# A hybrid attention block on one core: late weights split in place, eleven gate buffers, an earlier attention start and held transposes

## The chip, the cores and the metric

The kernel runs on 1 core of one Trainium2 chip. The metric is the device time of one execution in microseconds (us), the median over several runs. The engines are named as in the profile: PE (TensorE, matmuls) with PEld (its weight loads), DVE (VectorE), ACT (ScalarE), POOL (GpSimd), and SP (SyncE), on whose queue the kernel issues nearly all of its DMA transfers. Each engine works through its own instructions in order and waits for the others by semaphores.

## The reference

One layer over 2048 rows of 1024 numbers, float32. All inputs are projected at once, three branches follow, each with its own gate, and one output projection with a residual and a norm closes:

```python
h = rms_norm(x, norm_g)
z = h @ w_in
(aq, ak, av, af, az, bq, bk, bv, ba, bb, bz, mq, mz, gates) = _split_cols(z, IN_SIZES)
o_a = forgetting_attention(q, k, v, af + b_fg)          # 8 heads of 64, causal, 2048 x 2048
y_a = o_a * silu(az)
o_b = gated_delta_rule(gq, gk, gv, g_log, beta)         # 4 heads of 128, chunked scan
y_b = rms_norm(o_b, gdn_norm_g) * silu(bz)
y_m = memory_attention(mq, mem) * silu(mz)              # 4 heads of 128 over 256 memory rows
proj = einsum('bsnc,ncd->bsnd', [y_a, y_b, y_m], w_branch)   # 3 x (512 -> 1024)
merged = sum_n sigmoid(gates + b_merge)_n * proj_n
return rms_norm(x + merged @ w_out, final_norm_g)
```

## The kernel before

Every large product is made in three matmuls: each float32 operand is split into a rounded high part and its residue (names ending in `h` and `l`), and high x high, high x residue and residue x high are added in PSUM. The split of a tile is a copy to the high part on ScalarE and a subtraction into the residue on VectorE or POOL.

**Who sets the order.** The program is written by generators ("parts") that yield the time at which their next step may run. A class `Plan` (L25) keeps a modelled time for each engine, the SP queue and the transfers, and always takes the first part that is ready by that model; the dense products come last in the list and fill what is left. What is issued this way then stands in each engine's instruction stream, with some reordering by the layer below. `pl.at(t, f)` runs `f` at a modelled time, `Feed` (L109) keeps a limited number of loads under way, `Stores` (L132) issues stores late, and `behind(engine)` places a step directly after that engine's last instruction. On the chip the order stands and only the waits differ.

**The stages.**
1. `part_norm` (L503) norms the rows of `x` and turns them with PE transposes into `hh`/`hl`, the operands of all input products. The first 512 rows come in two pairs of 128-row tiles (`rms_transposed`, L332, once for `v` = 0 and 1). Beside them `dense` (L1492) starts the first two weight columns on half the rows at a time: `pdf` of pair 0, then of pair 1. The transposes (`ptx`, L371) go to a ring of three PSUM buffers; ScalarE copies a half tile to `hh` (L373), VectorE takes the residue to `hl` (L374), which frees the buffer.
2. `dense` then goes through 64 more columns of `w_in` (`pd_in`, L412 to 414), with the memory branch, the delta rule and, at the end, attention beside it. The last 24 columns are the gates. They are made first for the lower half of the rows (`HA`), then for the upper half (`HB`), in pieces of 512 rows; `ev_gate` (L461) counts the pieces of the upper half in `gates_b` and stores each to DRAM (`dgt`).
3. `part_mem_attn` (L712) makes the memory branch's output, 16 pieces of 128 x 512, and stores each already split, as two tiles (`dym`).
4. `part_fox` (L1159) is the forgetting attention. It starts when the lower gates are done and `gates_b` is 6. `maxima` computes scores for the row maxima (`psm`, L1254), `values` the scores again (`pst`) and the value products (`po`, `pq`, L1413 and 1414); POOL adds up the probabilities (L1374). `prep` and `load_q` load keys, values and queries. The outputs go to `dya`.
5. After the gates, `dense` runs the branch products for the delta rule (`n` = 1) and the memory branch (`n` = 2), each for four row groups `g` of 512 and eight output columns `d` of 128: 64 steps of 12 matmuls (`pbr`, L1625 to 1627, in `branch`). Attention runs beside the first 57 or so. A step needs its weights (`W`), its inputs (`yh`/`yl`), a gate tile `gt` (loaded by `load_gate`, two steps ahead), and for `n` = 2 also the partial sum `pp` of `n` = 1. VectorE multiplies gate and product into `gt` (L1654), POOL adds `pp` (L1658), and `gt` is stored to DRAM (`dpt`) and only then free. Gate tiles have 5 buffers in one pool and, until step (2, 2), 5 more in a second pool `bx`; attention may end only after `bx` is closed.
6. `branch_half` (L1765) does the third branch (attention, `n` = 0) on 256 rows at a time, in pairs of columns (`pba`, L1785 to 1787), with a `gt` and a `pp` per pair, and leaves the merged sum in `mh`/`ml`; three PSUM buffers take turns. `out_half` (L1814) multiplies by `w_out` (`pout`, L1832 to 1834), adds the residual, and norms. The sequence is `branch_half(0)`, `branch_half(1)`, `out_half(0)`, `branch_half(2)`, `out_half(1)`, and so on.

**The late weights.** `w_branch` of attention and `w_out` are loaded and split around the passage from stage 5 to 6. `load_wb` for `n` = 0 loads a raw tile `wbr` from the input into one of four staging buffers (`yr`, two loads under way), casts it to `wbh` (L1579) and subtracts into `wbl` (L1580). `load_y1` stages attention's outputs in `yr` likewise. `load_wo` stages a row block of `w_out` in one of two buffers `ld3`, which the output stage's scratch `jk3` shares.

Of the kernel before, what the change touches and what calls it, by code (L numbers as in the profile page):

```python
# [19 lines left out]
P = 128  # L20
# [191 lines left out]
def tile_trunk(ctx, tc, x, mem, norm_g, w_in, w_v, w_lg, b_fg, b_mg, conv_w, a_log, dt_b,  # L212
# [65 lines left out]
    dwb = [dram.tile([P, 2, 8, 4, P], F32, name=f"dwb{n}") for n in range(3)]  # L278
    dF = dram.tile([2, 8, S], F32, name="dF")
# [45 lines left out]
    state = {"gates_a": False, "gates_b": 0, "fox": False, "wb": False, "bx": False, "pv": 0}  # L325
# [6 lines left out]
    def rms_transposed(pool, load, ntile, g_bc, hi, lo, col0, ring, batch, on_dve=(), parts=1):  # L332

        tend = 0.0
        for t0 in range(0, ntile, batch):
# [23 lines left out]
            for t in range(t0, t0 + batch):  # L359
# [4 lines left out]
                for hf in range(KT // 4):  # L364
                    yield later(t2, ring.when), 0.44
                    pt, kb = ring.take("ptx")
                    pt = four(pt)
                    with behind(mybir.EngineType.PE) if parts > 1 else nullcontext():
                        for a in range(4):
                            k = hf * 4 + a  # L370
                            nc.tensor.transpose(pt[:, a, :], xt[:, k * P:(k + 1) * P], ident)  # L371
# [131 lines left out]
    def part_norm():  # L503
        with tc.tile_pool(name="p0", bufs=2) as p0:
# [207 lines left out]
    def part_mem_attn(n, g, h, qh, ql, tq):  # L712
# [53 lines left out]
        yield later(e - AHEAD, lambda: 0.0 if mem_s["y"] == n else INF), 0.0  # L766
        yh = mp.tile([P, 512], F32, tag="yh", name="yh", bufs=1)
# [390 lines left out]

    def part_fox():  # L1159
        yield (lambda: 0.0 if state["gates_a"] and state["gates_b"] >= 6 else INF), 0.0  # L1160
        ps1.close()
        fs = ExitStack()
# [280 lines left out]
        yield (lambda: 0.0 if state["pv"] == NU and state["bx"] else INF), 0.0  # L1443
# [48 lines left out]
    def dense():  # L1492
        first = state["first"]
        ps0 = []
        for v in range(2):
            cs = slice(256 * v, 256 * v + 256)
            for i in range(2):
# [5 lines left out]
                for k in range(KT):  # L1503
                    mm3k(ps[:, cs], wh, wl, hh[0][:, :, cs], hl[0][:, :, cs], k)
                    if k < KT - 1:
                        yield 0.0, 0.34
                if v == 1:
# [43 lines left out]
        bs, bxs = ExitStack(), ExitStack()  # L1551
        bw = bs.enter_context(tc.tile_pool(name="bw", bufs=1, side="right"))
        bp = bs.enter_context(tc.tile_pool(name="bp", bufs=1, side="right"))
        bx = bxs.enter_context(tc.tile_pool(name="bx", bufs=1))
        src_y = [dya, dyb, dym]
        W = {}

        wb_feed, y_feed = Feed(pl, 2), Feed(pl, 2)

        def load_wb(n, d):  # L1560
# [24 lines left out]
        def load_y1(n, g, k):  # L1585
            cell = []
            if n:
# [319 lines left out]
```

## Time and profile before

| | us |
|---|---|
| median of 3 runs | 2618.22 |
| lowest and highest | 2616.93, 2618.88 |
| the profiled execution | 2617.02 |
| its span, first to last instruction | 2615.3 |
| PE busy in it | 2551.5 |
| POOL busy in it | 1016.9 |

The profile is that of one execution. "Busy" adds up the time in which an engine had an instruction under way. A row of a table by stretch gives the stretch, its length, the busy time of each engine with the number of its instructions, the mean granted clock of TensorE as a share of full speed, the mean busy share of the 16 DMA engines, and GB/s moved. In a timeline a row gives start, duration, engine, source line, operation, output and inputs, size and count, and in brackets the idle time before it with what ended it. Matmuls overlap, so their pace is the distance of starts, not the duration.

### The profile page before, as it was taken

The numbers are of one execution on the slowest core, as the hardware profiler recorded it, in microseconds if no ns is written. First come the engines' busy times: TensorE is split into PE (matmuls) and PEld (weight loads), VectorE is DVE, ScalarE is ACT, GpSimd is POOL, SyncE is SP. The second block draws the span as 40 slices with busy tenths as digits, with TensorE's granted clock in tenths as the row PEclk, the third lists the DMA queues.
The fourth block names the chain that finished last, engine by engine and source line by source line (L and its number), as shares of the span: only waits on it lengthen the run. The fifth ranks groups of instructions, "written<-read, shape, count | busy, mean of one in ns | idle before, by whom it ended". The sixth has DMA issues, their size and how long they took to land. (4 is left out here: it accounts for less than half of the span.)

```text
span 2615.3 us, 36792 instructions
## 1 busy us (share of the span) xinstructions
PE 2551.5 (98%) x12656; PEld 2110.6 (81%) x12656; DVE 1337.0 (51%) x2718; ACT 1103.8 (42%) x2296; POOL 1016.9 (39%) x819
## 2 busy tenths in 40 slices
PE   7999999999999999999999999999999999989998
PEld 6778888788888888888888888788887887768887
DVE  6641566656433337712222247666667776635433
ACT  5531234443475532234444335555565444422211
POOL 0011111221144334243333237777775657862111
PEclk9999999999999999999999999999999999999999
DMA  5123222222365665467665463443336787786332
GB/s 194 62 87 118 76 89 89 93 89 88 127 228 200 204 211 170 129 225 226 204 200 164 147 186 94 116 122 113 97 111 213 207 263 228 246 271 218 129 122 73
DMA packets 314986, 407.27 MB, mean 156 GB/s; under 512 B 63520, under 2 KB 186528, under 8 KB 314799
## 3 DMA queue, kind: packets, MB, share of 16 engines
q1 hardware_dynamic: 314654, 404.65, 48.4%
q8 instruction: 100, 1.64, 0.3%
q14 instruction: 88, 0.71, 0.1%
q10 hardware_dynamic: 144, 0.26, 0.0%
HBM read 246.13 MB, written 158.68 MB: 155 GB/s over the span
## 5 line engine op out<-in xcount | busy, mean ns | idle before, releaser
L412 PE MATMUL pd_in<-hh,wh_in 128*128 128x512 f32 x1856 | 746.1, 402 | 3.2 <-DVE evt L455 2.9
L414 PE MATMUL pd_in<-hh,wl_in 128*128 128x512 f32 x1856 | 728.4, 392 | 1.0
L413 PE MATMUL pd_in<-hl,wh_in 128*128 128x512 f32 x1856 | 726.1, 391 | 0.0
L396 POOL TENSOR_TENSOR wl_in<-wr_in,wh_in 128x1024 fp32r<-128x1024 f32 x84 | 203.9, 2427 | 644.3 <-ACT wh_in L392 633.2
L414 PEld LDWEIGHTS pd_in<-hh,wl_in 128*128 128x128 f32 x1856 | 348.8, 188 | 79.3 <-POOL wl_in L396 4.5
L412 PEld LDWEIGHTS pd_in<-hh,wh_in 128*128 128x128 f32 x1856 | 349.8, 188 | 71.7 <-DVE evt L455 4.3
L413 PEld LDWEIGHTS pd_in<-hl,wh_in 128*128 128x128 f32 x1856 | 350.1, 189 | 64.8
L1374 POOL TENSOR_TENSOR acc<-acc,ph 128x512 f32<-128x512 f32 (+3 forms) x288 | 318.7, 1107 | 75.4 <-ACT ph L1394 57.7
L1394 ACT ACTIVATE ph<-pst 128x512 fp32r<-128x512 f32 (+1 forms) x320 | 170.8, 534 | 183.9 <-PE pst L1388 92.6
L1351 DVE TENSOR_TENSOR plo<-pst,ph 128x512 fp32r<-128x512 f32 (+1 forms) x320 | 191.3, 606 | 83.1 <-ACT pst L1396 79.6
L1396 ACT ACTIVATE pst<-pst 128x512 f32<-128x512 f32 (+1 forms) x320 | 170.8, 534 | 0.0
L1658 POOL TENSOR_TENSOR gt<-gt,pp 128x512 f32<-128x512 f32 x64 | 87.4, 1370 | 180.2 <-DVE gt L1654 147.1
L392 ACT CAST wh_in<-wr_in 128x1024 fp32r<-128x1024 f32 x84 | 88.1, 1049 | 156.6 <-PE pd_in L413 138.7
L1261 DVE TENSOR_REDUCE nmx<-psm 128x1 f32<-128x512 f32 x192 | 128.0, 685 | 32.5 <-PE psm L1254 30.8
L1413 PE MATMUL po<-ph,Vs 128*128 128x512 f32 (+1 forms) x320 | 117.2, 368 | 2.3 <-ACT ph L1394 2.2
L1387 PE MATMUL pst<-QA,KA 128*128 128x512 f32 (+1 forms) x320 | 117.5, 367 | 2.0 <-DVE QA L1269 1.7
L486 DVE SCALAR_TENSOR_TENSOR evv<-xb,cw,evv 128x512 f32<-128x512 f32 x144 | 116.6, 809 | 3.7
L1414 PE MATMUL pq<-plo,Vs 128*128 128x512 f32 (+1 forms) x320 | 116.9, 367 | 0.7 <-DVE plo L1351 0.7
L1388 PE MATMUL pst<-QB,KB 128*128 128x512 f32 (+1 forms) x320 | 117.1, 367 | 0.0
L1254 PE MATMUL psm<-KA,QA 68*128 68x512 f32 (+2 forms) x320 | 109.6, 375 | 4.3 <-DVE nmx L1258 2.0
L1832 PE MATMUL pout<-woh,mh 128*128 128x512 f32 x256 | 101.1, 397 | 8.4 <-ACT mh L1758 6.5
L1625 PE MATMUL pbr<-yh,wbh 128*128 128x512 f32 x256 | 102.1, 399 | 5.9 <-DVE gt L1654 5.3
(353 smaller groups left out, 4750.0 us busy)
## 6 DMA issues: line engine op xcount, KB each, us to landing
wr_in<-in_w_in SPq DMA_DIRECT2D x84, 512.0 KB
dgt<-evg SPq DMA_DIRECT2D x96, 256.0 KB
gt<-dgt SPq DMA_DIRECT2D x96, 256.0 KB
dpt<-gt SPq DMA_DIRECT2D x64, 256.0 KB
pp<-dpt SPq DMA_DIRECT2D x64, 256.0 KB
dgq<-evv SPq DMA_DIRECT2D x48, 256.0 KB
kqv<-dgq SPq DMA_DIRECT2D x16, 768.0 KB
xt<-in_x SPq DMA_DIRECT2D x16, 512.0 KB
```

Of the source, the lines that this page charges most:

```text
L396: nc.gpsimd.tensor_sub(lo, raw, hi.bitcast(F32))
L412: nc.tensor.matmul(ps, wh[:, k, :], xh[:, k, :], start=(k == 0), stop=False)
L413: nc.tensor.matmul(ps, wh[:, k, :], xl[:, k, :], start=False, stop=False)
L414: nc.tensor.matmul(ps, wl[:, k, :], xh[:, k, :], start=False, stop=(k == kt - 1))
L1261: nc.vector.tensor_reduce(mx, ps[:, 0:w], AX.X, ALU.max)
L1351: nc.vector.tensor_sub(plo[:, 0:w], ps[:, 0:w], ph[:, 0:w].bitcast(F32))
L1374: nc.gpsimd.tensor_add(acc[:, c0:512], acc[:, c0:512], ph[:, 0:w].bitcast(F32))
L1387: nc.tensor.matmul(ps[:, 0:w], KA[kt][:, ks], QAn[:, c0:512], start=True, stop=False)
L1388: nc.tensor.matmul(ps[:, 0:w], KB[kt][:, ks], QBn[:, c0:512], start=False, stop=True)
L1394: nc.scalar.activation(ph[:, 0:w], ps[:, 0:w], AF.Exp, scale=0.125)
L1396: nc.scalar.activation(ps[:, 0:w], ps[:, 0:w], AF.Exp, scale=0.125)
L1413: nc.tensor.matmul(po[:, c0:512], V[:, 0:128], ph[:, 0:w], start=(t0 == 0), stop=(t0 == NT - 1))
```

## The change

Seven edits go together:

- The transposes of the second pair of tiles are held until both `pdf` products of the first pair have been issued (`turn`, `state["pair"]`), and placed right behind PE's last instruction.
- For the last row group, the memory branch stores its output whole. `load_y1` splits it when it is loaded.
- `part_copy`, started with attention, copies attention's `w_branch` and `w_out` from the inputs to DRAM tiles `dw0` and `dwo`, one block of each at a time, 30 us of modelled time apart.
- Attention starts when `gates_b` is 3, and its end no longer waits for `bx`.
- Late weights, attention's outputs and the last memory group land in the residue's tile (`wbl`, `wol`, `yl`); ScalarE casts from there to the high part and the residue is subtracted in place. The staging buffers and their feeds go.
- Gate tiles have 11 buffers in one pool from first to last; `bx` is gone.
- `w_out` blocks are asked for two at first, then one with each pair of columns of `branch_half`. `jk3` has a buffer of its own.

```diff
+    def part_copy():
+
+        for d in range(8):
+            with behind(mybir.EngineType.SP):
+                move(dw0[:, d], w_br[0, d], 512)
+                move(dwo[d], w_out[d], 1024)
+            yield pl.pe + 30.0, 0.0
+
     def part_fox():
-        yield (lambda: 0.0 if state["gates_a"] and state["gates_b"] >= 6 else INF), 0.0
+        yield (lambda: 0.0 if state["gates_a"] and state["gates_b"] >= 3 else INF), 0.0
         ps1.close()
+        pl.add(part_copy())
...
-        yield (lambda: 0.0 if state["pv"] == NU and state["bx"] else INF), 0.0
+        yield (lambda: 0.0 if state["pv"] == NU else INF), 0.0
...
-                    yield later(t2, ring.when), 0.44
+                    yield later(t2, ring.when, turn or 0.0), 0.44
...
-                    with behind(mybir.EngineType.PE) if parts > 1 else nullcontext():
+                    with behind(mybir.EngineType.PE) if parts > 1 or turn else nullcontext():
...
+            first_pair = lambda: 0.0 if state["pair"] == 2 else INF
...
-                                                     256 * v, rc, 1, (1,))
+                                                     256 * v, rc, 1, (1,), turn=first_pair if v else None)
...
+        if g == NG - 1:
+            yield e, 0.0
+            move(dym[g][:, h, 0, :], zm, 256, e)
+            mem_s["left"] -= 1
+            mem_s["y"] = n + 1
+            return
...
-            def load():
-                raw = bp.tile([P, 4, P], F32, tag="yr", name="wbr", bufs=4)
-                return raw, move(raw, w_br[n, d], 256)
-
-            def use(raw):
-                hi, lo = tiles()
-                nc.scalar.copy(hi, raw)
-                nc.gpsimd.tensor_sub(lo, raw, hi.bitcast(F32))
+            hi, lo = tiles()
+            t = move(lo.bitcast(F32), dw0[:, d], 256)
+
+            def use():
+                nc.scalar.copy(hi, lo.bitcast(F32))
+                nc.gpsimd.tensor_sub(lo, lo.bitcast(F32), hi.bitcast(F32))
                 cell.extend((hi, lo, pl.pool(512, pl.act(512, pl.pe))))

-            wb_feed.ask(load, use)
+            pl.at(t, use)
...
-            if n:
-                hi = bp.tile([P, 512], F32R, tag="yh", name="yh", bufs=YB)
-                lo = bp.tile([P, 512], F32R, tag="yl", name="yl", bufs=YB)
+            hi = bp.tile([P, 512], F32R, tag="yh", name="yh", bufs=YB)
+            lo = bp.tile([P, 512], F32R, tag="yl", name="yl", bufs=YB)
+            if n and (n, g) != (2, NG - 1):
...
+            t = move(lo.bitcast(F32), src_y[n][g][:, k, 0, :] if n else src_y[n][g][:, k, :], 256)
+            pl.at(t, lambda: cell.extend((hi, lo, split(hi, lo, lo.bitcast(F32), 512, pl.pe))))
             return cell
...
-        YB, GB, GX = 8, 5, 5
+        YB, GB = 8, 11
...
-                wide = n == 1 or g < NG // 2
-                parts.leave(GB + GX * wide - 3)
-                pool, bufs = next(turn) if wide else (bp, GB)
-                gt = pool.tile([P, 512], F32, tag="gt", name="gt", bufs=bufs)
+                parts.leave(GB - 3)
+                gt = bp.tile([P, 512], F32, tag="gt", name="gt", bufs=GB)
...
-            def load():
-                raw = f3.tile([P, D], F32, tag="ld3", name="wor", bufs=2)
-                return raw, move(raw, w_out[k], 512)
+            woh, wol = F["woh"], F["wol"]
+            raw = wol[:, k].bitcast(F32)
+            t = move(raw, dwo[k], 512)
...
-                for k in range(KT):
-                    load_wo(k)
+                for _ in range(2):
+                    load_wo(ks.popleft())
...
-            if (n, g) == (2, NG // 2):
-                parts.leave(0)
-                bxs.close()
-                state["bx"] = True
...
                     load_pair(*todo.popleft())
+                if ks:
+                    load_wo(ks.popleft())
...
-                        jk = f3.tile([P, D], F32, tag="ld3", name="jk3", bufs=2)
+                        jk = f3.tile([P, D], F32, name="jk3", tag="jk3")
```

More of the change, by code (lines that the diff above doesn't have):

```diff
@@ L278, in tile_trunk @@
     dwb = [dram.tile([P, 2, 8, 4, P], F32, name=f"dwb{n}") for n in range(3)]
+    dw0 = dram.tile([P, 8, 4, P], F32, name="dw0")
+    dwo = [dram.tile([P, D], F32, name=f"dwo{k}") for k in range(8)]
     dF = dram.tile([2, 8, S], F32, name="dF")
@@ L324, in tile_trunk @@
     hhalf = [INF] * 2
-    state = {"gates_a": False, "gates_b": 0, "fox": False, "wb": False, "bx": False, "pv": 0}
+    state = {"pair": 0, "gates_a": False, "gates_b": 0, "fox": False, "wb": False, "pv": 0}
     done = {}
@@ L330, in load_x, with rms_transposed @@
         return xt, move(xt, src[row: row + P, :], 512)
-    def rms_transposed(pool, load, ntile, g_bc, hi, lo, col0, ring, batch, on_dve=(), parts=1):
+    def rms_transposed(pool, load, ntile, g_bc, hi, lo, col0, ring, batch, on_dve=(), parts=1, turn=None):
         tend = 0.0
@@ L1506, in dense @@
                         yield 0.0, 0.34
+                state["pair"] += 1
                 if v == 1:
@@ L1592, in load_y1 @@
                 return cell
-            def load():
-                raw = bp.tile([P, 512], F32, tag="yr", name="yr", bufs=4)
-                return raw, move(raw, src_y[n][g][:, k, :], 256)
-            def use(raw):
-                hi = bp.tile([P, 512], F32R, tag="yh", name="yh", bufs=YB)
-                lo = bp.tile([P, 512], F32R, tag="yl", name="yl", bufs=YB)
-                cell.extend((hi, lo, split(hi, lo, raw, 512, pl.pe)))
-            y_feed.ask(load, use)
+            t = move(lo.bitcast(F32), src_y[n][g][:, k, 0, :] if n else src_y[n][g][:, k, :], 256)
+            pl.at(t, lambda: cell.extend((hi, lo, split(hi, lo, lo.bitcast(F32), 512, pl.pe))))
             return cell
@@ L1632, in branch @@
                     mid()
-        gates, parts, turn = {}, Stores(pl), itertools.cycle([(bp, GB)] * GB + [(bx, GX)] * GX)
+        gates, parts = {}, Stores(pl)
         def load_gate(n, g, d, ahead=0):
             if (n, g, d) not in gates:
-                wide = n == 1 or g < NG // 2
-                parts.leave(GB + GX * wide - 3)
-                pool, bufs = next(turn) if wide else (bp, GB)
-                gt = pool.tile([P, 512], F32, tag="gt", name="gt", bufs=bufs)
+                parts.leave(GB - 3)
+                gt = bp.tile([P, 512], F32, tag="gt", name="gt", bufs=GB)
                 move(gt, dgt[g][:, n * 8 + d, :], 256)
@@ L1665, in ev_dram, with use @@
             return e
-        F, wo, wo_feed = {}, {}, Feed(pl, 2)
+        F, wo, ks = {}, {}, collections.deque(range(KT))
         def load_wo(k):
-            f3, woh, wol = (F[n] for n in ("f3", "woh", "wol"))
-            def load():
-                raw = f3.tile([P, D], F32, tag="ld3", name="wor", bufs=2)
-                return raw, move(raw, w_out[k], 512)
-            def use(raw):
+            woh, wol = F["woh"], F["wol"]
+            raw = wol[:, k].bitcast(F32)
+            t = move(raw, dwo[k], 512)
+            def use():
                 nc.scalar.copy(woh[:, k], raw)
@@ L1681, in use @@
                 wo[k] = pl.pool(D, t) if k % 2 else pl.dve(D, t)
-            wo_feed.ask(load, use)
+            pl.at(t, use)
         def open_out():
@@ L1838, in out_half @@
                     if jk is None:
[L1839 removed]
+                        jk = f3.tile([P, D], F32, name="jk3", tag="jk3")
                     nc.scalar.activation(jk[:, cs], xt[:, cs], AF.Square, accum_out=s2[:, hf:hf + 1], scale=D ** -0.5)
                     if row == S - P and not hf:
[L1842 removed]
+                        xf = jk[:, cs]
                         nc.gpsimd.tensor_mul(xf, xt[:, cs], fg[:, cs])
[L1844 removed]
                     e = pl.act(512, e)
```

6 lines of the change are left out of this document (1 added, 5 removed).

## The prediction

> **What bounds the kernel now.** I read the page first, then the stretches by engine, the waits of TensorE, and the timelines of the two places where it stands.
>
> ```profile
> span 2615.3 us, 36792 instructions
> PE 2551.5 (98%) x12656; PEld 2110.6 (81%) x12656; DVE 1337.0 (51%) x2718; ACT 1103.8 (42%) x2296; POOL 1016.9 (39%) x819
> core 0: us, PE busy (x) PEld busy (x) DVE busy (x) ACT busy (x) POOL busy (x), PEclk, DMA share, GB/s
> 1546.00:1990.00 444.00, 439.81 (x2015) 359.60 (x2013) 297.62 (x679) 257.19 (x507) 318.26 (x268) 1.00 0.38 113
> 2162.00:2255.00 93.00, 90.40 (x395) 71.28 (x393) 65.98 (x142) 42.34 (x90) 72.13 (x65) 0.98 0.74 226
> 2255.00:2295.00 40.00, 37.15 (x161) 29.29 (x161) 23.14 (x41) 16.89 (x34) 33.65 (x29) 1.00 0.68 227
> 2295.00:2321.00 26.00, 23.30 (x98) 18.21 (x99) 13.81 (x13) 3.73 (x6) 19.14 (x16) 1.00 0.87 287
> 2321.00:2350.00 29.00, 19.97 (x104) 16.31 (x103) 9.12 (x11) 9.58 (x13) 15.04 (x11) 0.82 0.90 300
> 2350.00:2378.00 28.00, 26.02 (x163) 23.23 (x162) 15.36 (x17) 9.83 (x14) 14.84 (x9) 0.94 0.74 242
> 2378.00:2600.00 222.00, 220.17 (x1242) 193.91 (x1241) 91.30 (x190) 44.83 (x107) 33.61 (x24) 1.00 0.39 129
> ```
>
> TensorE works in 98% of the span, and the change leaves its matmuls as many as they were. Only its idle time, 2615.3 - 2551.5 = 63.8 us, and its time at a lower clock can go. The rows show where that is: attention beside the gates (1546 to 1990) idles 4.2 us in 444, the last stage 1.8 in 222. The last branch steps (2295 to 2321) idle 2.7 in 26, and the passage from them to the output stage (2321 to 2378) 9.0 + 2.0 = 11.0 us, at a granted clock of 0.82 and 0.94, which takes 0.18 x 29 + 0.06 x 28 = 6.9 us more. The passage loses 17.9 us, the largest sum in one place that the change touches.
>
> Who ends these waits (us, times, longest):
>
> ```profile
> PE pout L1832 <- ACT mh L1758: 6.5, 1, 6.5
> PE pbr L1625 <- DVE gt L1654: 5.3, 7, 1.6
> PE ptx L371 <- DVE hl L374: 4.3, 5, 2.5
> PE pout L1833 <- POOL wol L1680: 1.9, 1, 1.9
> ```
>
> **The change part by part.**
>
> *Held transposes.* Before, on TensorE and VectorE at the start:
>
> ```profile
> 38.66 4.05 PE L371 MATMUL ptx<-ident,xt 128*128 128x128 f32 x20 [2.50 <-DVE hl L374]
> 43.68 0.73 PE L412 MATMUL pdf<-hh,wh_in 128*128 128x512 f32 x2 [0.97 <-ACT hh L373]
> 37.32 0.69 DVE L444 TENSOR_TENSOR evl<-pdf,evh 128x512 fp32r<-128x512 f32 x1 [0.65 <-DMA dqh<-evh]
> 37.92 1.87 DVE L374 TENSOR_TENSOR hl<-ptx,hh 128x512 fp32r<-128x512 f32 x3
> ```
>
> The order moves 6 matmuls ahead of the second pair's 16 transposes, which is nothing by itself. What counts is VectorE: the first `hl` of the next group stood behind the second `evl`, which waited for a store and came at 37.32. Now it stands between the two, so it can end some 2 us sooner, and the transposes that wait 2.50 us for its buffer with it. The cost may be that four halves share three buffers. I take -1.5 us, from -3 (the 2.50 and some of the 0.97 go) to +1 (one more turn of ScalarE and VectorE before the next matmul).
>
> VectorE, before and then after (line numbers are two higher after):
>
> ```order
> L374 TENSOR_TENSOR hl_276<-ptx,hh_272 128x4x128 x2
> L362 SCALAR_TENSOR_TENSOR xt<-xt,rs,g_bc 128x1024 x3
> L444 TENSOR_TENSOR evl<-pdf_0_387,evh 128x512
> L362 SCALAR_TENSOR_TENSOR xt<-xt,rs,g_bc 128x1024
> L444 TENSOR_TENSOR evl<-pdf_0_419,evh 128x512
> L374 TENSOR_TENSOR hl_277<-ptx,hh_273 128x4x128 x8
> ```
>
> ```order
> L376 TENSOR_TENSOR hl_285<-ptx,hh_281 128x4x128 x4
> L364 SCALAR_TENSOR_TENSOR xt<-xt,rs,g_bc 128x1024 x4
> L446 TENSOR_TENSOR evl<-pdf_0_396,evh 128x512
> L376 TENSOR_TENSOR hl_286<-ptx,hh_282 128x4x128
> L446 TENSOR_TENSOR evl<-pdf_0_428,evh 128x512
> L376 TENSOR_TENSOR hl_286<-ptx,hh_282 128x4x128 x7
> ```
>
> One `hl` of the second group has moved ahead of the waiting `evl`.
>
> *Attention three gate pieces in, not six.* On TensorE at attention's start (`psm` are its first scores), before and then after:
>
> ```order
> L412 MATMUL pd_in_2_3_12867<-hh_275,wh_in_2_12706 128x512
> L413 MATMUL pd_in_2_3_12867<-hl_279,wh_in_2_12706 128x512
> L414 MATMUL pd_in_2_3_12867<-hh_275,wl_in_2_12708 128x512
> L1254 MATMUL psm<-KA_12745,QA_12757 128x128
> L1254 MATMUL psm<-KA_12745,QA_12757 128x256
> ```
>
> ```order
> L414 MATMUL pd_in_2_3_12800<-hh_284,wh_in_2_12637 128x512
> L415 MATMUL pd_in_2_3_12800<-hl_288,wh_in_2_12637 128x512
> L416 MATMUL pd_in_2_3_12800<-hh_284,wl_in_2_12639 128x512
> L1272 MATMUL psm<-KA_12650,QA_12662 128x128
> L1272 MATMUL psm<-KA_12650,QA_12662 128x256
> ```
>
> The first score stands 57 gate matmuls earlier: at 23.30 / 98 = 0.238 us each (the 2295 row) 13.6 us. What it needs is there by then:
>
> ```profile
> 1546.49 0.57 PE L1254 MATMUL psm<-KA,QA 68*128 68x128 f32 x3
> 1530.69 0.26 DVE L1202 MEMSET mt<- 128x100 f32 x2
> ```
>
> 1546.5 - 13.6 = 1532.9, after attention's last memset at 1530.95. So the move is free, with 2 us to spare. It changes the end: behind attention's last value product stood 111 branch matmuls (9 steps of 12), now 216 (18 steps). By itself it moves time and saves none.
>
> *The copies.* Eight pairs of DRAM-to-DRAM transfers (256 and 512 KB), issued on SP some 30 us apart beside attention. The cover is the DMA share of 0.38 in the 1546 row; no row prices such a copy. I take 0, since 8 x 0.79 MB spread over 444 us adds 14 GB/s to 113. If each pair holds up what is queued behind it for 0.79 MB / 300 GB/s = 2.6 us, that is 21 us on the queue; a third of it on TensorE, 7, is the upper end (more is a rival below). A gain is excluded: nothing leaves the queue.
>
> *Eleven gate buffers; branch steps.* The last steps now, by line:
>
> ```profile
> L1625 PE MATMUL pbr<-yh,wbh 128*128 128x512 f32 x32 | 13.0, 405 | 3.6 <-DVE gt L1654 3.6
> L1658 POOL TENSOR_TENSOR gt<-gt,pp 128x512 f32<-128x512 f32 x10 | 12.8, 1291 | 3.8 <-DMA pp<-dpt 3.2 <-issue 0.6
> L1654 DVE SCALAR_TENSOR_TENSOR gt<-gt,pbr 128x512 f32<-128x512 f32 x9 | 5.9, 675 | 10.7 <-DMA gt<-dgt 8.1 <-PE pbr L1627 2.6
> gt<-dgt SPq DMA_DIRECT2D x96, 256.0 KB
> dpt<-gt SPq DMA_DIRECT2D x64, 256.0 KB
> pp<-dpt SPq DMA_DIRECT2D x64, 256.0 KB
> ```
>
> VectorE waits 8.1 us there for gates, whose load waits for one of 5 buffers to be stored. With 11 that goes, and the 5.3 us of TensorE behind it. What is late next is the transfers themselves. A step moves 3 x 256 KB. The last 16 steps now run without attention: 16 x 12 x 0.238 = 45.7 us. They move 16 x 3 x 256 KB, less 4 loads that come before them and 4 stores that come after, plus 8 inputs `y` and 5 weights of 256 KB and 2 of 512 KB: 57 x 256 KB = 14.9 MB, or 327 GB/s. The 2321 row shows 300 at a share of 0.90: 14.9 / 0.300 = 49.8 us, 4.1 late; at the 287 of the row before 6.4 late; at 333 (300 / 0.90) nothing. I take +4, so -5.3 + 4 = -1.3 us, from -5.3 to +1.1.
> The Trainium skill (DMA: Bandwidth & Descriptors, Specifications) puts a core's share of the memory at about 358 GB/s; by that the steps are not held up and the sum below is 4 us lower. No stretch here shows it held for 30 us, so I go by the rows.
>
> *Weights split in place; the passage.* Before:
>
> ```profile
> 2340.10 0.79 PE L1832 MATMUL pout<-woh,mh 128*128 128x512 f32 x1 [6.47 <-ACT mh L1758]
> 2322.31 0.32 SPq L244 DMA_DIRECT2D gt<-dgt  x1
> 2323.22 0.53 SPq L244 DMA_DIRECT2D pp<-dpt  x1
> 2329.79 1.12 SPq L244 DMA_DIRECT2D gt<-dgt  x1
> 2325.70 0.69 DVE L1654 SCALAR_TENSOR_TENSOR gt<-gt,pbr 128x512 f32<-128x512 f32 x1 [0.75 <-DMA gt<-dgt]
> 2328.13 1.27 POOL L1658 TENSOR_TENSOR gt<-gt,pp 128x512 f32<-128x512 f32 x1 [3.77 <-DMA wbr<-in_w_br]
> 2337.36 0.69 DVE L1654 SCALAR_TENSOR_TENSOR gt<-gt,pba 128x512 f32<-128x512 f32 x1 [2.32 <-POOL wol L1680]
> ```
>
> The last branch matmul ends where the 2321 row begins (call it 0). Its gate is issued only at +1.3, `pp` at +2.2, POOL adds at +7.1, the store follows, and behind it on SP the first pair's gate at +8.8, which VectorE uses from +16.4 to 17.0; `pout` starts 2.05 us after that. SP's queue, before and then after:
>
> ```order
> L244 DMA gt<-dgt_118 128x512
> L244 DMA dya_122<-oT 64x512
> L244 DMA pp<-dpt_3_138 128x512
> L244 DMA wbr<-in_w_br 128x512 x2
> L244 DMA wor<-in_w_out 128x1024 x2
> L244 DMA dpt_3_134<-gt 128x512 x4
> L244 DMA gt<-dgt_115 128x2x256
> ```
>
> ```order
> L244 DMA gt<-dgt_118 128x512
> L244 DMA dpt_3_134<-gt 128x512
> L244 DMA wbl_21529<-dw_142 128x512
> L244 DMA wol<-dwo_143 128x1024
> L244 DMA wol<-dwo_144 128x1024
> L244 DMA pp<-dpt_3_138 128x512
> L244 DMA dpt_3_134<-gt 128x512
> L244 DMA wbl_21554<-dw_142 128x512
> L244 DMA dpt_3_134<-gt 128x512
> L244 DMA wbl_21573<-dw_142 128x512
> L244 DMA dpt_3_134<-gt 128x512 x2
> L244 DMA gt<-dgt_115 128x2x256
> ```
>
> The last gate now needs no store before it, and 1 MB of output weights goes out ahead of the last `pp`, not behind it. The pair loads still stand behind the last stores. With `pp` issued at 0 and as long on its way as now (2328.13 - 2323.22 = 4.9 us), POOL adds from +4.9 to 6.2 and the pair's gate goes out at +6.7. It took 7.6 us (2337.36 - 2329.79) behind weights and stores; I take 5, near the 4.9 of `pp`, as a megabyte less stands ahead: VectorE is done with it at +12.4, 4.6 us sooner. TensorE's pace meanwhile:
>
> ```profile
> 2326.43 0.28 PE L1785 MATMUL pba<-yh,wbh 128*128 128x256 f32 x1
> 2326.55 0.28 PE L1786 MATMUL pba<-yl,wbh 128*128 128x256 f32 x1
> ```
>
> Three product buffers hold 72 matmuls of 0.12 us: 8.6 us. A weight split in place cannot be loaded before the old one is read, where one of two spare buffers took it in earlier; 1 us of waits for that makes +9.6. Then 2.8 for the buffer, 12 matmuls to +13.8, 0.6 for the first `mh` (12.4 + 2.05), and the 1.9 for `wol`: 6.3 us for 11.0. For the clock:
>
> ```profile
> 2187.19 0.50 PE L1413 MATMUL po<-ph,Vs 128*128 128x512 f32 x1 [0.55 <-ACT ph L1394]
> 2188.39 0.45 PE L1254 MATMUL psm<-KA,QA 68*128 68x384 f32 x1 [0.58 <-DVE nmx L1258]
> 2189.44 0.63 PE L1388 MATMUL pst<-QB,KB 128*128 128x512 f32 x1
> 2189.87 0.63 PE L1414 MATMUL pq<-plo,Vs 128*128 128x512 f32 x1
> ```
>
> After two gaps of under 0.6 us matmuls start 0.43 us apart, not 0.24, so short gaps can cost clock too. In proportion to the idle time 4.0 of the 6.9 us would stay; I keep 2.7, since the long gap goes. The passage: -(17.9 - 6.3 - 2.7) = -8.9 us, from -14 (only the 1.9 and 2 us stay) to -2 (all as late as now, but for the clock).
> The Trainium skill (TensorE: Matmul & The Clock Gate, Why this matters for your kernels) warns of gaps over about 3 us; by that the passage keeps no clock loss and the sum is 2.7 us lower. The rows above speak against it.
>
> The last memory group stored whole and split later, and the single `jk3`, cost 0: they take 4 splits off ScalarE and POOL at a time when neither bounds, and put 4 on ScalarE and VectorE at step 50, where VectorE works 13.81 of 26 us; without that cover 4 x 0.7 us.
>
> The sum: -1.5 + 0 + 0 - 1.3 - 8.9 = -11.7 us.
>
> **Rivals.**
> *The transfers bind* (to no change): without attention between them the steps run at 287 GB/s, 6.4 us late, and carry the backlog into the passage, which gains only 2. -1.5 + 1.1 - 2 = -2.4. For it: SP's queue is in order and `pp` has 3 buffers still. Against: the 2255 row shows 227 GB/s, room just ahead.
> *The transfers have room*: no delay in the steps, and pair loads 2 us sooner. -1.5 - 5.3 - 10.9 = -17.7. For it: while TensorE stood, the engines moved 300 GB/s at 0.90 of their time, so not all of it.
> The Trainium skill (DMA: Bandwidth & Descriptors, Specifications) would have it so, by the figure cited above.
> *The copies stall attention* (slower): each pair takes the engines 5.2 us (read and write counted apart) and the keys, queries or values behind it come late by as much, at 8 places: +42 - 11.7 = +30 us; it decides once loads have less than 5 us to spare. Against: none of TensorE's waits is for a load of attention.
> *The waits don't move*: eleven buffers, but loads are still asked for two steps ahead only, and `pp` binds. The steps gain nothing and the passage 4: -5.5.
>
> **How the numbers follow.** The profiled execution took 2617.02 us, 1.7 over its span; the median of the runs is 2618.22, 1.2 above it. The forecast: 2617.0 - 11.7 + 1.2 = 2606.5 us, chance 0.40. The rivals, from the median: bind 2615.8, 0.18; room 2600.5, 0.20; stall 2648, 0.08; don't move 2612.7, 0.10; the rest, small losses, 0.04. A measurement of this kernel can tell about 0.2%, 5.2 us, from no change: under 2613.0 is faster, over 2623.5 slower. Faster: forecast, room, and half of don't move, which lies on the edge: 0.65. Same: bind and the other half, 0.23. Slower: stall and the rest, 0.12. The range takes in room with 5 us under it, bind with 3 above it, and leaves out stall, the rest, and the corner where every term is at its bound (from -3 - 5.3 - 14 = -22 to +1 + 7 + 1.1 - 2 = +7): 2595 to 2619.
>
> **What would show it.** Start: the first 512-wide `pdf` near 42 us, not 43.68. Attention: first `psm` near 1533, 216 branch matmuls behind its end. Steps: no wait of VectorE for `gt`; over 4 us for `pp` or `gt` at a DMA rate under 300 is *bind*. Passage: first `pout` waits under 3 us, clock over 0.9, VectorE at the first pair by +12. Wrong: the 6.5 us still there, or TensorE's score and value matmuls waiting for loads of `KA`, `QA` or `Vs` every 30 us.

## The result, and the profile after

The changed kernel takes 2604.55 us (median of 6 runs, 2602.25 to 2609.40) against 2618.38 for the kernel before (6 runs, 2616.93 to 2619.89). The ratio is 0.9945, 95% interval 0.9934 to 0.9955: 0.55% faster. The forecast was 2606.5 (2595 to 2619). The sum came out near the time, in part by luck: two of its terms are wrong and cancel each other.

The three rows below are stretches of the kernel before, cut where the same work is done: up to the 4001st matmul of the input columns, from there to the first `pba`, and the rest (columns as in the prediction).

```profile
0.00:1346.92 1346.92, 1319.80 (x6540) 1087.91 (x6541) 638.58 (x1226) 563.21 (x1207) 348.95 (x262) 1.00 0.45 148
1346.92:2321.09 974.17, 958.17 (x4582) 783.43 (x4580) 578.79 (x1266) 473.96 (x949) 603.27 (x515) 1.00 0.54 168
2321.09:2615.30 294.21, 273.50 (x1537) 239.22 (x1535) 119.63 (x226) 66.61 (x140) 64.68 (x44) 0.97 0.46 153
```

The same three stretches of the changed kernel:

```profile
0.00:1344.62 1344.62, 1318.82 (x6540) 1087.30 (x6541) 635.81 (x1226) 560.20 (x1203) 344.50 (x258) 1.00 0.45 147
1344.62:2316.57 971.95, 956.22 (x4582) 786.87 (x4581) 584.79 (x1272) 476.65 (x955) 604.75 (x516) 0.99 0.57 175
2316.57:2603.50 286.93, 271.55 (x1537) 238.57 (x1535) 118.55 (x224) 65.48 (x138) 64.59 (x43) 0.98 0.45 151
```

TensorE issues the same number of matmuls in each. The first stretch became 2.3 us shorter (forecast: 1.5), the second 2.2 (forecast: 1.3), the end 7.3 (forecast: 8.9).

TensorE's waits in the changed kernel (total, times, longest) that answer to the four shown of before:

```profile
PE pbr L1630 <- DVE gt L1657: 8.9, 4, 5.9
PE ptx L373 <- DVE hl L376: 4.4, 7, 1.5
PE pba L1786 <- POOL wbl L1594: 3.3, 2, 2.2
PE pout L1832 <- POOL wol L1681: 2.3, 2, 1.9
PE pout L1831 <- ACT woh L1678: 2.0, 1, 2.0
```

The 6.5 us of `pout` for `mh` are gone. In the branch steps the waits behind VectorE did not go. They grew from 5.3 to 8.9, and one alone is 5.93 us, in a place where the kernel before had none over 1.6. The timelines around it, TensorE first, then ScalarE and VectorE, then SP's queue and POOL some 20 us earlier:

```profile
2279.65 0.79 PE L1630 MATMUL pbr<-yh,wbh 128*128 128x512 f32 x1 [5.93 <-DVE gt L1657]
2273.62 0.62 ACT L642 CAST yh<-yl 128x512 fp32r<-128x512 f32 x1 [13.77 <-DMA yl<-dym]
2267.84 0.69 DVE L1657 SCALAR_TENSOR_TENSOR gt<-gt,pbr 128x512 f32<-128x512 f32 x1 [2.03 <-PE pbr L1632]
2274.27 0.69 DVE L643 TENSOR_TENSOR yl<-yl,yh 128x512 fp32r<-128x512 f32 x1 [5.74 <-ACT yh L642]
2275.71 3.35 DVE L1327 RECIPROCAL den<-den 64x512 f32<-64x512 f32 x1
2278.98 1.21 DVE L1657 SCALAR_TENSOR_TENSOR gt<-gt,pbr 128x512 f32<-128x512 f32 x2
2252.02 0.46 SPq L244 DMA_DIRECT2D gt<-dgt  x1
2258.32 0.32 SPq L244 DMA_DIRECT2D pp<-dpt  x1
2267.36 0.32 SPq L244 DMA_DIRECT2D yl<-dym  x1
2268.69 1.76 SPq L244 DMA_DIRECT2D yl<-dym  x3
2251.11 5.93 POOL L1392 TENSOR_TENSOR acc<-acc,ph 128x512 f32<-128x512 f32 x5
2257.00 1.29 POOL L1661 TENSOR_TENSOR gt<-gt,pp 128x512 f32<-128x512 f32 x1
```

Read it from the VectorE rows. After the product at 2267.84 VectorE's next instruction is the residue of a `yl` of the last memory group, the group that the change stores whole and splits when it is loaded. It waits 5.74 us, because ScalarE's cast waits for the load. The steps' gate products stand behind it, and behind a reciprocal of 3.35 us; they come at 2278.98. They alone free TensorE's two product buffers. A second wait of the same kind follows at 2308.1: TensorE stands 2.31 us for a product that VectorE reaches late, because it waited 4.25 us for one of attention's outputs, split in the same way. The four loads went out from 2267.36 on. SP's queue had stood from 2252.5 to 2258.3, while POOL had 5.93 us of attention's additions ahead of the one that frees a `pp`. The stretches of 5 us show that stand as empty engines, and behind the stall a lower clock:

```profile
2255.00:2260.00 5.00, 5.00 (x26) 4.17 (x25) 1.02 (x3) 1.11 (x2) 4.11 (x6) 1.00 0.08 26
2270.00:2275.00 5.00, 3.73 (x17) 2.75 (x15) 0.70 (x2) 0.69 (x2) 0.86 (x1) 1.00 1.02 381
2275.00:2280.00 5.00, 0.35 (x1) 0.35 (x2) 4.96 (x4) 1.78 (x3) 0.80 (x1) 0.58 0.65 238
2280.00:2285.00 5.00, 5.00 (x18) 3.98 (x18) 5.00 (x5) 0.00 (x0) 3.27 (x3) 0.74 0.44 124
```

5.93 us of wait and 0.26 x 5 = 1.3 us of clock in the last row: some 7 us that the forecast did not have. The experiments begin there.

### The profile page after: what moved, and what is told of

Its sections match the earlier page's. It is cut to its first block, busy times and chain, and to the rows that moved or that the text cites. A ratio compares the mean times of both kernels' runs of the same rounds, so it can differ in the third digit from the quotient of the medians.

```text
span 2603.5 us, 36786 instructions
## 1 busy us (share of the span) xinstructions
PE 2546.6 (98%) x12656; PEld 2112.7 (81%) x12656; DVE 1339.2 (51%) x2722; ACT 1102.3 (42%) x2296; POOL 1013.8 (39%) x815
## 5 line engine op out<-in xcount | busy, mean ns | idle before, releaser
L1630 PE MATMUL pbr<-yh,wbh 128*128 128x512 f32 x256 | 103.6, 405 | 9.2 <-DVE gt L1657 8.9
L1832 PE MATMUL pout<-wol,mh 128*128 128x512 f32 x256 | 100.5, 393 | 2.4 <-POOL wol L1681 2.3
```

The costliest lines, as they stand in the source:

```text
L1832: nc.tensor.matmul(ps, mh[:, k, ts], wol[:, k, cs], start=False, stop=False)
```

## The experiments

Twelve kernels, each timed beside the kernel before on the same chip. That kernel took 2622.7, 2624.4 and 2622.6 us there, not 2618.4, so ratios are compared, and the times expected are read as shares of 2618.4. The changed kernel was not timed again on those chips, so its ratio stands beside ratios from other chips. The stages are read from TensorE's matmuls in each profile: the start until the first `pd_in`, from there to the end of the span, the 384 matmuls of the memory branch (from the first `pbr` of `n` = 2 to the first `pba`), and the passage (first `pba` to first `pout`).

| kernel | ratio (95% interval) | first `pd_in` | from there to the end | `n` = 2 | passage |
|---|---|---|---|---|---|
| before | 1 | 103.5 | 2511.8 | 159.0 | 19.0 |
| changed | 0.9945 (0.9934 to 0.9955) | 103.0 | 2500.5 | 130.9 | 14.1 |
| memory group stored split | 0.9909 (0.9896 to 0.9923) | 101.2 | 2494.1 | 121.5 | 15.6 |
| no held transposes | 0.9946 (0.9934 to 0.9959) | 103.6 | 2500.2 | 131.8 | 14.1 |
| attention after 6 pieces | 0.9915 (0.9901 to 0.9928) | 105.5 | 2494.3 | 134.5 | 18.8 |
| 5 gate buffers | 0.9951 (0.9939 to 0.9964) | 101.0 | 2506.7 | 134.9 | 16.3 |
| stored split, 6 pieces | 0.9916 (0.9902 to 0.9929) | 102.6 | 2498.7 | 143.4 | 15.5 |
| copies twice | 0.9908 (0.9894 to 0.9921) | 101.5 | 2495.7 | 130.5 | 13.8 |
| stored split, `wol` on VectorE | 0.9890 (0.9876 to 0.9903) | 101.2 | 2489.5 | 122.2 | 14.0 |
| stored split, pairs first | 0.9895 (0.9881 to 0.9909) | 102.7 | 2490.0 | 121.8 | 12.4 |
| all three of these | 0.9902 (0.9888 to 0.9915) | 103.4 | 2493.5 | 121.6 | 11.6 |
| all of `w_out` at once | 0.9948 (0.9934 to 0.9961) | 104.4 | 2507.3 | 135.4 | 22.1 |
| 4 `pp`, 10 gate buffers | 0.9935 (0.9923 to 0.9947) | 101.6 | 2501.1 | 129.7 | 11.5 |
| stored split, weights staged | 0.9917 (0.9903 to 0.9932) | 101.1 | 2492.2 | 124.1 | 15.0 |

How far may such numbers be trusted? In the eleven of these kernels that start attention after three pieces, TensorE's order from the 4001st input matmul to the first `pbr` of `n` = 2 is the changed kernel's, yet that stretch took from 837.5 us (copies twice) to 845.0 (all three), one profile each. One stretch of it in both, first in the slower, then in the faster:

```profile
1650.00:1700.00 50.00, 47.70 (x214) 38.78 (x213) 31.54 (x78) 25.16 (x51) 36.08 (x30) 0.97 0.36 107
```

```profile
1650.00:1700.00 50.00, 50.00 (x231) 41.19 (x231) 34.89 (x84) 27.73 (x54) 38.61 (x32) 1.00 0.53 162
```

A wait of TensorE for VectorE of some 2 us, and the lower clock behind it, come in one execution and not in the other. So the total of one profile says little below 7 us, and the five executions of the last kernel of the table lie 9.5 us apart (2595.03 to 2604.56). The last two columns say more: from the first `pbr` of `n` = 2 to the first `pout`, TensorE's instructions are the same in all eleven. (The two kernels with six pieces and the one before still have attention's among them, and the one before has 72 `pba` in the passage, not 84.) The ratios have their own limit: "copies twice", an edit that was expected to change nothing, came out 0.0037 under the changed kernel, and no run tells why. A ratio that differs from the changed kernel's by that much does not name its cause; a wait that comes or goes in the profile has to.

**1. The memory group stored split, as before.**

```diff
-        if g == NG - 1:
-            yield e, 0.0
-            move(dym[g][:, h, 0, :], zm, 256, e)
...
-            if n and (n, g) != (2, NG - 1):
+            if n:
...
```

> The changed kernel, but the last memory group is stored already split, as before the change, and loaded as two tiles; TensorE's instructions stand in the same order. In the changed kernel VectorE stood 5.74 us for a yl of that group (2268.5 to 2274.3), the gate product stood behind it, and TensorE waited 5.93 us. Theory, the split blocks: without it that wait and the 1.3 us of lower clock behind it go, 7 us: about 2597.5 (2595 to 2600). Rival, the loads bind: the eight loads in place of four bring 1 MB more into a stretch that moved 362 to 381 GB/s, TensorE waits for them or for pp instead, and no more than 2 us are gained: 2602 to 2605.

Ratio 0.9909 (the theory's 2595 to 2600 are 0.991 to 0.993, the rival's 2602 to 2605 are 0.994 to 0.995), and the memory branch takes 121.5 us for 130.9. TensorE's wait for VectorE in the steps:

```profile
PE pbr L1624 <- DVE gt L1651: 1.4, 3, 0.6
```

And a stretch of the steps in which it does not wait at all:

```profile
2275.00:2307.00 32.00, 32.00 (x143) 26.46 (x142) 11.80 (x15) 4.96 (x8) 20.48 (x17) 1.00 1.04 384
```

The split was the stall, and that does not rest on one profile. Five kernels load the group whole, start attention after three pieces and keep at least ten gate buffers (changed, no held transposes, copies twice, all of `w_out`, 4 `pp`): TensorE's longest wait for a gate product in their steps is 5.05 to 6.58 us, and their memory branch takes 129.7 to 135.4 us. In the five that store it split and start attention as early, no such wait is longer than 2.01 us, and the branch takes 121.5 to 124.1. Of the 9.4 us between the two kernels compared here 8.9 - 1.4 = 7.5 are such waits, and 1.3 the clock behind the longest. The rival falls, and with it a second idea of the forecast: with 1 MB more to move, the engines carried 384 GB/s for 32 us while TensorE worked without a gap.

**2. Without the held transposes.**

```diff
-                                                     256 * v, rc, 1, (1,), turn=first_pair if v else None)
+                                                     256 * v, rc, 1, (1,), turn=None)
```

> The changed kernel without the held transposes. In the traces so far the 1000th matmul of the input columns came 2.0 us earlier after the change: 0.5 us until the last pdf, and 1.5 us between 110 and 150 us, where the granted clock was 0.96 before and 1.00 after. Theory, the hold gives only 0.5 us and the clock is a matter of where a gap falls: the last pdf comes 0.5 us later, and of the 1.5 us some or none: 0.5 to 2 us slower, 2605 to 2606.6. Rival, the hold gives the 1.5 us that the prediction took for the start, all of it before the last pdf: the last pdf 1.5 us later.

Ratio 0.9946 against 0.9945: no difference that can be measured. The last `pdf` comes 0.57 us later (103.33 for 102.76), which is the theory's 0.5 in this one pair of profiles. The first 512-wide `pdf`, in the changed kernel, in this one, and in the one with attention after 6 pieces, which holds the transposes too:

```profile
43.13 0.87 PE L414 MATMUL pdf<-hh,wh_in 128*128 128x512 f32 x2
```

```profile
43.72 0.73 PE L414 MATMUL pdf<-hh,wh_in 128*128 128x512 f32 x2 [0.99 <-ACT hh L375]
```

```profile
45.01 1.22 PE L414 MATMUL pdf<-hh,wh_in 128*128 128x512 f32 x2
```

In the twelve profiles with the hold it starts between 41.2 and 45.0 us, in the two without at 43.68 and 43.72. Ten of the twelve are earlier than that, so 1 to 2 us may well be gained, but the same order gives 3.8 us of spread. The theory's 0.5 us stands within that; the 1.5 us that it put down to the clock (261.6 us for 263.1 from the first to the 1001st input matmul) turn up in ten of the twelve profiles with the hold and in neither without, and the runs here do not settle which it is. The wait itself did not go: up to 42 us TensorE waits once for `hl` without the hold, 2.62 us; in the changed kernel three times, 0.53 + 0.60 + 1.48 = 2.61 us.

**3. Attention after six pieces.**

```diff
-        yield (lambda: 0.0 if state["gates_a"] and state["gates_b"] >= 3 else INF), 0.0
+        yield (lambda: 0.0 if state["gates_a"] and state["gates_b"] >= 6 else INF), 0.0
```

> The changed kernel, but attention starts after 6 gate pieces, as before the change; 156 branch matmuls stand behind the last value product in place of 216. Theory, the early start moves time and saves none: within 2 us of the changed kernel, 2602.5 to 2606.5. Rival, the pure steps at the end pay for their transfers, so fewer of them are better: 3 to 6 us faster, 2599 to 2601.5. Second rival, the early start is what keeps the end fed: 4 us slower or more, over 2608.5.

Ratio 0.9915, faster than the changed kernel and beyond the rival's 0.993 (though not by more than "copies twice", which should change nothing). Its waits in the steps:

```profile
PE pbr L1630 <- DMA yh<-dyb: 3.9, 1, 3.9
PE pbr L1630 <- DVE gt L1657: 1.1, 2, 0.6
```

The 5.93 us are not there. VectorE has attention's work until 2277.6 us, and when it comes to the split of the memory group it waits 0.57 us, not 5.74:

```profile
2282.12 2.71 DVE L643 TENSOR_TENSOR yl<-yl,yh 128x512 fp32r<-128x512 f32 x4 [0.57 <-ACT yh L642]
```

So the early start does not only move time: it brings that stall about. What it costs in all is less sure. The passage is back at 18.8 us for 14.1, so part is given back.

**4. Five gate buffers.**

```diff
-        YB, GB = 8, 11
+        YB, GB = 8, 5
```

> The changed kernel with 5 gate buffers from first to last in place of 11; TensorE's order is the same. Theory, the eleven buffers give the 5.3 us of waits for gates in the branch steps and part of the passage: 5 to 10 us slower, 2610 to 2615. Rival, the transfers and VectorE's splits set the pace of the last steps and the buffers are worth little: within 2.5 us, 2602 to 2607.

The ratio is 0.9951, 0.0006 above the changed kernel's, which is the rival's band (0.994 to 0.996); its profile says 6.2 us in the whole, 4.0 in the memory branch and 2.3 in the passage, which is the theory's. Both cannot hold. What VectorE's gate products waited for, from 2262 us to the end of the steps, shows the mechanism:

```profile
L1657 DVE SCALAR_TENSOR_TENSOR gt<-gt,pbr 128x512 f32<-128x512 f32 x15 | 10.0, 678 | 16.6 <-DMA gt<-dgt 5.8 <-POOL wbl L1594 5.0 <-PE pbr L1632 5.0
```

In the changed kernel no gate product waits for a gate there. The eleven buffers take those waits away, as forecast; what that is worth lies between 1 and 6 us. (TensorE's longest wait in this kernel's steps, 5.18 us at 2302.5, stands behind another split: VectorE waited 7.18 us for a `yl` of attention's outputs.)

**5. Stored split and six pieces together.** The edits of 1 and 3.

> Both of the earlier single edits on the changed kernel: attention starts after 6 gate pieces, and the last memory group is stored already split. Counted from the first matmul of the input columns to the end of the span, since the start differs by up to 4 us between executions: before 2511.8, changed 2500.5, either edit alone 2494.1 and 2494.3. Theory, it is one and the same stall (with attention beside them the loads land before VectorE comes to their split): 2494 again, within 2 us. Rival, two separate gains: the late start gives 6 us by having fewer pure steps, and the sum is about 2488.

Ratio 0.9916, the same as either alone: no second gain. The profile, 2498.7 us, fits neither number, for a wait that neither theory had:

```profile
2275.33 0.69 DVE L1651 SCALAR_TENSOR_TENSOR gt<-gt,pbr 128x512 f32<-128x512 f32 x1 [2.15 <-DMA gt<-dgt]
2281.12 0.68 DVE L1318 TENSOR_TENSOR den<-pL,oT 64x512 f32<-64x512 f32 x1 [5.10 <-PE pL L1307]
2281.84 3.35 DVE L1321 RECIPROCAL den<-den 64x512 f32<-64x512 f32 x1
2285.11 1.21 DVE L1651 SCALAR_TENSOR_TENSOR gt<-gt,pbr 128x512 f32<-128x512 f32 x2
2285.78 0.79 PE L1624 MATMUL pbr<-yh,wbh 128*128 128x512 f32 x1 [4.70 <-DVE gt L1651]
```

It is the same pattern with another cause: here VectorE's order put attention's last division ahead of two gate products; the division waits for a matmul that TensorE reaches two steps later, and TensorE then waits 4.70 us for the products.

**6. Every copy twice.**

```diff
                 move(dwo[d], w_out[d], 1024)
+                nc.sync.dma_start(dx0[:, d], w_br[0, d])
+                nc.sync.dma_start(dxo[d], w_out[d])
```

> The changed kernel with each of the sixteen copies from DRAM to DRAM made twice (the second one to tiles that nobody reads); TensorE's order is the same. Theory, the copies are hidden: counted from the first matmul of the input columns, 2500.5 within 2 us, and no wait of TensorE in attention for keys, queries or values. Rival, a copy holds the transfers behind it up: 7 us or more slower, 2507 or more.

Not slower, and TensorE waits for no key, query or value in attention: the copies are hidden. That it came out faster (0.9908), as much as experiment 1, stays unexplained; 3.5 of the 4.8 us by which its profile is shorter lie in the attention stretch that varies by 7.5 us anyway.

**7 and 8. Two edits in the passage, on top of experiment 1.** The second block of `w_out` split on VectorE:

```diff
-                lo = nc.gpsimd if k % 2 else nc.vector
+                lo = nc.gpsimd if k % 2 and k > 1 else nc.vector
...
```

> The kernel with the last memory group stored split (2494.1 us from the first matmul of the input columns), and the second block of w_out split on VectorE in place of POOL. There POOL subtracted that block from 2313.73 to 2316.10 with a subtraction of wbl behind it, for which TensorE waited 2.55 us in the passage. Theory, POOL's queue sets that wait: it goes, and part of the 1.9 us of pout for wol: 2 to 4 us faster, 2490 to 2492. Rival, the pairs' gates, which VectorE awaits until 2319.2, set the passage: the wait moves behind them, under 1 us.

The first two pairs' loads ahead of the last two stores:

```diff
-        parts.leave(0)
...
         for _ in range(2):
+            parts.leave(GB - 3)
             load_pair(*todo.popleft())
+        parts.leave(0)
```

> The kernel with the last memory group stored split (2494.1 us from the first matmul of the input columns), and the loads of the first two pairs of the attention branch issued ahead of the last two stores of the branch steps, which held SP for 4.9 us there (2309.2 to 2314.1). Theory, that hold sets when the first output product can start: the first pout, 15.6 us after the first pba now, comes 3 to 4 us sooner and the whole 2 to 4 us: 2490 to 2492. Rival, TensorE's wait for wbl (2.55 us) and the three product buffers set it: under 1 us.

Ratios 0.9890 and 0.9895; the profiles land at the theories' 2490 or just under it. In the passage itself the first is worth 1.5 us (15.6 to 14.0; TensorE's wait for `wbl` falls from 2.55 to 1.01), the second 3.2 (to 12.4). The second theory holds; the first edit lies between its theory (2 to 4 us) and its rival (under 1). Neither ratio is clear of experiment 1's 0.9909.

**9. All three.**

> Three edits on the changed kernel together: the last memory group stored split, the first two pairs' loads ahead of the last two stores, and the second block of w_out split on VectorE. Singly, on top of the first, the other two took the stretch from the first pba to the first pout from 15.6 us to 12.35 (pair loads) and 14.0 (split on VectorE). Theory, the two waits lie one behind the other (1.60 us for wbl is left with the pair loads early): about 11 us for the stretch, and 0.9885 of the kernel before, about 2593 us on this chip's like. Rival, they cover each other: 12.3 us again and no faster than either.

The passage takes 11.6 us, 0.8 less than with the pairs alone: between theory and rival. The whole, 0.9902, is not the theory's 0.9885, and no faster than 7 or 8; its attention stretch was the longest of all, 845.0 us. All three beat the changed kernel; which of 7, 8 and 9 is best these runs do not tell.

**10. All of `w_out` at once.**

```diff
-                for _ in range(2):
+                for _ in range(KT):
                     load_wo(ks.popleft())
```

> The changed kernel, but all eight blocks of w_out are asked for at once, ahead of the last pp of the branch steps, in place of two and then one with each pair: 3 MB more stand in front of the last pp and the pair loads. Theory, what stands ahead of the pair loads in the queue sets the first output product: at 350 GB/s the 3 MB take 9 us, and the stretch from the first pba to the first pout, 14.1 us in the changed kernel, takes 19 to 23; later the 2.3 us of waits for wol go; together 3 to 8 us slower. Rival, the engines take later transfers beside earlier ones and the pairs come nearly as early: within 2 us.

The passage takes 22.1 us for 14.1, inside the theory's 19 to 23. The output stage then gets 7.6 us back (214.0 for 221.6 us from the first `pout` to the last `pba`), and the ratio, 0.9948, is not clear of the changed kernel's, where the theory had 3 to 8 us. Nor is the path quite the theory's. The first `pout` waits for nothing; before it TensorE waits for attention's `w_branch`:

```profile
2336.93 0.58 PE L1784 MATMUL pba<-yh,wbh 128*128 128x256 f32 x1 [5.25 <-ACT wbh L1593]
2341.59 0.58 PE L1786 MATMUL pba<-yh,wbl 128*128 128x256 f32 x1 [3.86 <-POOL wbl L1594]
2336.26 0.62 ACT L1593 CAST wbh<-wbl 128x512 fp32r<-128x512 f32 x1 [0.94 <-DMA wbl<-dw]
2326.77 9.03 POOL L1681 TENSOR_TENSOR wol<-wol,woh 128x1024 fp32r<-128x1024 f32 x3 [1.59 <-ACT woh L1678]
```

That weight's load went out at 2326.97, behind the eight blocks, and took some 9 us. Then its residue stood on POOL behind the subtractions of `w_out`. So what stands ahead in the queue does set the passage, but by way of the weights, and POOL's row adds to it. TensorE has other work later, and most of the time comes back.

**11. Four buffers for `pp`, ten for gates in place of eleven.**

> The changed kernel with 4 buffers for pp and 10 gate buffers. SP stood from 2252.5 to 2258.3 for one of three pp buffers, whose addition on POOL stood behind 5.9 us of attention's additions, and the transfers ran at a share of 0.08 from 2255 to 2260; the yl of the last memory group, whose split held VectorE up for 5.74 us, were issued at 2267.4 to 2270.4. Theory, that stand makes the yl late: it goes or shortens, and TensorE's 5.93 us fall to 3 or less: 3 to 6 us faster from the first branch matmul of n = 2 (at 2185.6) to the first pba, 130.9 us now. Rival, the store behind it waits for the same addition, so the queue stands as long: the 5.93 us stay within 1 us.

TensorE's wait is 5.05 us, the rival's "within 1 us". SP's queue now stands a few places later, for 4.9 us:

```profile
2255.28 0.43 SPq L244 DMA_DIRECT2D gt<-dgt  x1
2260.62 0.32 SPq L244 DMA_DIRECT2D pp<-dpt  x1
```

One more `pp` buffer does not help here: the queue stands until POOL's addition at 2259.30 is done, behind 5.96 us of attention's. The passage is 2.6 us shorter, which neither theory had, and the ratio, 0.9935, is not clear of the changed kernel's.

**12. Attention's weights staged again, on top of experiment 1**, with 7 gate buffers.

```diff
-            hi, lo = tiles()
-            t = move(lo.bitcast(F32), dw0[:, d], 256)
+            raw = bp.tile([P, 4, P], F32, tag="yr", name="wbr", bufs=4)
+            t = move(raw, dw0[:, d], 256)
...
```

> The kernel with the last memory group stored split, and attention's w_branch landing in four staging buffers again, as before the change, not in the residue's tile; 7 gate buffers in place of 11, whose room the staging takes. In it TensorE waited 2.55 us for wbl in the passage and the first pout came 15.6 us after the first pba. Theory, the landing in place costs little: the subtractions on POOL stand in the same row, so 15.6 within 1.5 us. Rival, the landing in place makes the weights late (it cannot start before the old weight is read): 2 to 3 us sooner.

The passage takes 15.0 us for 15.6, TensorE's wait for `wbl` 2.06 us for 2.55: the landing in place costs half a microsecond, unless the fewer gate buffers hide more. Experiment 7 took more off that wait (to 1.01) by taking one block out of POOL's row: the wait is mostly that row, and not the landing.

## Why the prediction was right, and where it was not

**Held transposes, -1.5 us.** The first stretch came out 2.3 us shorter, but equal orders differ by more, and the run without the hold is as fast. The forecast's own sign, the first 512-wide `pdf` near 42 us, came at 43.13, and the 2.50 us wait for `hl` was divided into three that add up to as much. The gain is not shown; the way to it, as forecast, did not come about.

**Attention three pieces in, 0.** The first score came at 1531.46 us (forecast: near 1533), with 216 branch matmuls behind the last value product. "By itself it moves time and saves none" failed: undoing it takes the 5.93 us stall away, and the ratio falls by 0.0030. With attention out of the way VectorE comes to the memory group's split before its loads are there.

**Copies, 0.** Right within what the runs can tell.

**Branch steps, -1.3 = -5.3 + 4.** The gate waits went, as forecast, but the 4 us for transfers that cannot keep up did not come: I took 300 to 333 GB/s as the limit from the passage, and experiment 1 shows 384 at a share of 1.04. The Trainium skill (DMA: Bandwidth & Descriptors, Specifications) gives about 358 GB/s as a core's share. The Trainium skill (Perfetto Trace Analysis, Roofline) says that a core which alone is active may exceed that share, up to about 435; the 384 agree with the second and lie above the first.

**Last memory group, 0, or 4 x 0.7 us without cover.** This is the step that failed. I counted the work of four subtractions, 0.69 us each. What they cost is their wait: an instruction that waits 5.74 us for a load, in VectorE's row ahead of the products that free TensorE's buffers. At the start of the kernel the prediction had named what stands behind a waiting instruction; it did not do so in the one place where the change adds such a wait. 7 us missed here, against 4 us too much for transfers and some 4 us of gain that the runs do not place (attention's stretch alone varies by 7.5), gave -2.2 for the stretch in place of -1.3: a near number from two wrong terms, and that is luck.

**The passage, -8.9.** The mechanism held, the size less. VectorE had the first pair at +11.4 us (2327.28 + 0.69 - 2316.57; forecast +12.4) and the first `pout` came at +14.1. The stretch that the forecast priced, up to the third half group:

```profile
2316.57:2368.99 52.42, 44.47 (x266) 39.12 (x265) 26.67 (x29) 19.63 (x28) 30.04 (x18) 0.93 0.85 297
```

In it, VectorE's first pair and three waits of TensorE:

```profile
2327.28 0.69 DVE L1657 SCALAR_TENSOR_TENSOR gt<-gt,pba 128x512 f32<-128x512 f32 x1 [5.66 <-DMA gt<-dgt]
2326.38 0.39 PE L1786 MATMUL pba<-yh,wbl 128*128 128x256 f32 x1 [2.23 <-POOL wbl L1594]
2351.44 0.50 PE L1831 MATMUL pout<-woh,mh 128*128 128x512 f32 x1 [2.00 <-ACT woh L1678]
2353.87 0.50 PE L1832 MATMUL pout<-wol,mh 128*128 128x512 f32 x1 [1.93 <-POOL wol L1681]
```

It took 57.15 us before (2321.09 to 2378.24) and 52.42 now: 4.7 us less, not 8.9. TensorE idles 7.95 us in it (forecast 6.3): `wbl` made it wait 2.23 + 1.12 where I allowed 1, since POOL takes a block of `w_out` first, and `woh` 2.00 where I allowed nothing. At a clock of 0.93 it loses 0.07 x 52.42 = 3.7 us more (forecast 2.7). The forecast's 17.9 us for the passage before was too large as well, because its two sums overlap: 4.27 us of the time at half clock lay inside the 6.47 us wait, where there was no matmul to slow down.

```profile
2335.83:2340.10 4.27, 0.00 (x0) 0.00 (x0) 1.39 (x3) 0.63 (x1) 3.25 (x3) 0.50 0.92 305
```

That is 2.1 us counted twice, so 15.8 us were lost before, not 17.9. Another 2.5 us came after that stretch (237.06 to 234.51), which I had not priced; 1.8 of it is one wait of `pout` for an `x` at 2380.7, which the changed kernel does not have.

**The rivals.** *Room* had the transfers right; with the memory group's split undone the kernel runs at 0.9909, 6 us under the 2600.5 of that rival. *Bind* and *stall* are refuted: 384 GB/s, and no wait in attention for a key, query or value. *Don't move* missed in its sum (2612.7), and VectorE's waits for gates did go; but its two signs are partly there: SP's queue stood 5.8 us for a `pp` buffer, and the stretch that the forecast priced gained 4.7 us, near the 4 of that rival.

## What to carry to other kernels

Price an instruction that you add to an engine's row by what it may wait for, not by how long it runs: name the load that it needs, when that load is issued, and what stands behind it. A split that ran late on the engine that also empties PSUM cost 7 us here; stored early, for 1 MB more to load, it cost nothing that these runs show. And where a change makes one stretch denser, look for the loads that were in time only because that stretch was slow, as the memory group's loads were with attention beside them.

## What the runs showed of the hardware that was not expected

Transfers kept 384 GB/s over 32 us, at a DMA share of 1.04 (experiment 1). And the clock can fall after gaps under 3 us, in the changed kernel's passage right behind the 2.23 us one:

```profile
2326.72 0.28 PE L1785 MATMUL pba<-yl,wbh 128*128 128x256 f32 x1
2326.84 0.32 PE L1786 MATMUL pba<-yh,wbl 128*128 128x256 f32 x1
2326.97 0.41 PE L1784 MATMUL pba<-yh,wbh 128*128 128x256 f32 x1
2327.17 0.41 PE L1785 MATMUL pba<-yl,wbh 128*128 128x256 f32 x1
```

The distance of the starts goes from 0.12 to 0.21 us. It need not fall: the last branch steps of the kernel before (2295 to 2321) had waits of 1.21 and 1.58 us at a clock of 1.00. By the rule of the Trainium skill that the prediction cited (TensorE: Matmul & The Clock Gate, Why this matters for your kernels) the passage, whose longest gap is 2.23 us, would have kept no clock loss; the trace disagrees, at 3.7 us.
